# A single-core hybrid HGRN2 / Conformer layer: measured durations in the planner's estimate, side taps held back while a root is pending, statistics delayed, final_g loaded with the last split of weights

## The chip, the cores and the metric

One core of one Trainium2 chip. The metric is the device time of one execution in microseconds, as the median of several runs. A profiled execution gives the rows that are quoted here.

## The reference

One decoder layer and a final norm, in float32, for 2048 new prompt tokens (16 meta tokens go ahead of them; their rows are dropped from the output) and one new token for each of 8 running sequences:

```python
hn = rmsnorm(h, norm1_g)
q_r, f_r, i_r, g_r, a_r, b_r = split(hn @ w_in)            # 1024 -> 4 x 512 and 2 x 512
f = lb + (1 - lb) * sigmoid(f_r)
o = hgrn2(silu(q_r), 1 - f, i_r, log(f))                   # 4 heads of 128 x 128 state, gated recurrence
y_hg = rmsnorm(o, hg_onorm_g) * silu(g_r)
glu = a_r * sigmoid(b_r)
y_cv = silu(layernorm(depthwise_conv31(glu) + conv_b))     # 512 channels
h = h + concat(y_hg, y_cv) @ w_out
h = h + square(relu(rmsnorm(h, norm2_g) @ w_up)) @ w_down  # 1024 -> 4096 -> 1024
y = rmsnorm(h, final_g)
```

The outputs are y for the prompt and for the samples, and the new recurrent and convolution states of both.

## The kernel before

Tokens lie along the free dimension of the matmuls, and channels on the partitions. The float32 products of the projections are formed from three products of parts: each factor is split into a high and a low part (hi and lo), and hi x hi, hi x lo and lo x hi are added in PSUM.

The prompt is cut into four quarters of 512 tokens. The first 950 us or so are a list of units on TensorE: the input projection of a quarter (24 units of 24 matmuls: q, f, v, g for each of four heads, a and b for each of four groups of conv channels) and the output projection of a quarter (8 units of 24 matmuls, one for each 128 of the 1024 columns), in the order in 0, in 1, out 0, in 2, out 1, in 3, out 2, out 3. The epilogue of a unit reads PSUM on ScalarE and VectorE. Then the MLP goes over the tokens in three passes of 680, 688 and 680, each with 16 groups of 256 hidden columns; the up projection of a group is formed from seven products of sums of blocks, and the pieces of the down projection lie between them.

All other work is done by *background generators*, which put their instructions between those of the units:

- `x_pair` and `x_work` (lines 417 and 435) load and transpose the tokens of a half quarter; x_pair finds the row norms (ScalarE squares, a root) and broadcasts them with a matmul of a diagonal tile (`dg`) against ones.
- `hgrn` (line 1002) is the chunked recurrence of one head in one quarter: a scan and a reciprocal on VectorE, transposes, score and state matmuls on PE, a root for the head's norm, a scaling on ScalarE (tile KPn), its transposes, and the split of the result into hi and lo. `hgrn_sample` does the samples.
- `conv` and `conv_part` (lines 1194 and 1206) add 31 taps for each channel group. VectorE takes taps from the front of the list into PSUM (`ps<-glu,cw,ps`), and the *side* takes them from the back: ScalarE multiplies (`acc<-glu,cw`) and POOL adds (`acc<-acc`). `ln_tiles` (line 1285) is the LayerNorm behind it.
- `out_store` (line 1438) stores a finished column block of h and adds up its squares (tile fg: ScalarE squares, POOL adds); behind the last block a matmul of ones with the sum (`fg,ones` on PE) gives the statistics of the MLP's norm. `h_first` and `h_rest` prepare the MLP's input.
- `finish` and `finish_last` (lines 1719 and 1750) end the MLP for up to 128 tokens: PE transposes the sum (`ident,acc`) into two PSUM banks, ScalarE adds up the squares (tile junk), POOL forms the root, VectorE scales with `final_g` (`xn<-ps,kept,fg`), which frees the banks.

A *root* is `rsqrt` (line 333): one VectorE operation, then a power on POOL (`kept<-stat,mhalf`), then back to the users.

Where a generator's steps come between the units is fixed when the program is built, by a planner. Every instruction goes through `Proxy.call` (lines 106 to 149; all show as line 147 in the profile), which adds an estimated cost to the clock of its engine in `Model`. A generator yields the name of the engine that its next step needs, and `Background.ready` (line 184) lets it go on when the estimate says so: a PE step when its inputs will be ready 60 ns before PE comes to it, a step of another engine when that isn't planned over 600 ns ahead, and a side tap when ScalarE and POOL aren't planned over 1500 ns ahead. Where a unit can't go on without a result, `Background.until` forces the steps that are left. The estimate sets the order only; on the chip the engines wait for each other by semaphores.

In the MLP, `d_load` and `d_split` (lines 1884 and 1900) load the down weights and split them in the first pass; the splits are kept in HBM (down_w) for the other passes. `to_store` holds DMA issues on SP back to a later unit. The tile `fg` takes a part of these weights while they are split, so final_g can be loaded into it only behind that.

## Time and profile before

| | before |
|---|---|
| median of 3 runs | 2393.43 us (2393.3 to 2396.77) |
| profiled execution, its own time | 2392.3 us |
| its span, first to last instruction | 2390.6 us (1.7 us lie around it) |
| mean granted clock of TensorE | 0.984 |
| busy: PE / DVE / ACT / POOL | 2280.4 / 1631.1 / 1047.1 / 693.4 us |

In the profile, PE is TensorE, DVE VectorE, ACT ScalarE, POOL GpSimd and SP SyncE. A row of the timeline says when an operation starts, how long it and those of its kind right behind it take, what it writes and reads (out<-in, the program's names without buffer numbers), its shape, and in brackets how long the engine idled before it, and on whom. A view of waits adds up such idle time by what ended it. The granted clock is the share of full speed at which TensorE may run.

### The profile page before, as it was taken

The numbers are of one execution on the slowest core, as the hardware profiler recorded it, in microseconds if no ns is written. First come the engines' busy times: TensorE is split into PE (matmuls) and PEld (weight loads), VectorE is DVE, ScalarE is ACT, GpSimd is POOL, SyncE is SP. The second block draws the span as 40 slices with busy tenths as digits, with TensorE's granted clock in tenths as the row PEclk, the third lists the DMA queues.
The fourth block names the chain that finished last, engine by engine and source line by source line (L and its number), as shares of the span: only waits on it lengthen the run. The fifth ranks groups of instructions, "written<-read, shape, count | busy, mean of one in ns | idle before, by whom it ended". The sixth has DMA issues, their size and how long they took to land.

```text
span 2390.6 us, 36863 instructions
## 1 busy us (share of the span) xinstructions
PE 2280.4 (95%) x13790; PEld 2141.5 (90%) x13790; DVE 1631.1 (68%) x2550; ACT 1047.1 (44%) x2195; POOL 693.4 (29%) x555
## 2 busy tenths in 40 slices
PE   8988989999998998999999998999999989999998
PEld 7987778878877886899999997999999989999998
DVE  5896977387559445577777765787776558666665
ACT  6543744454246242644554444344443353333332
POOL 4652543444147022253333331211111013100000
PEclk9998999999999999999999999999999999999999
DMA  8765445944664457456666575455554755333332
GB/s 298 243 209 168 171 182 176 329 161 158 208 216 163 143 212 261 136 182 185 200 201 195 166 241 183 156 166 173 169 164 122 235 177 162 111 110 111 111 110 108
DMA packets 309466, 428.68 MB, mean 179 GB/s; under 512 B 21506, under 2 KB 216391, under 8 KB 292896
## 3 DMA queue, kind: packets, MB, share of 16 engines
q1 hardware_dynamic: 309144, 426.06, 55.2%
q8 instruction: 109, 1.79, 0.3%
q14 instruction: 69, 0.57, 0.1%
q10 hardware_dynamic: 144, 0.26, 0.0%
HBM read 311.75 MB, written 114.97 MB: 179 GB/s over the span
## 4 chain that ended last, share of the span: by engine, by line
PE 61%; DVE 12%; DMA 5%; issue 4%; ACT 4%; POOL 1%; SPq 1%; POOLq 0%; ACTq 0%; DVEq 0%
PE ps L147 61%; DVE ps L147 4%; ACT cst L147 1%; DVE raw L147 1%; DVE cst L147 1%; SPq L147 1%; ACT wsp L147 1%; DMA xscr<-acc 1%; DVE acc L147 1%; DMA bst<-in_w_up_dram 1%; DMA junk<-in_w_down_dram 1%; DMA fg<-in_w_down_dram 1%; POOL wsp L147 1%; DMA bop_d<-stg 1%; DMA down_w<-wsp 1%
## 5 line engine op out<-in xcount | busy, mean ns | idle before, releaser
L147 PE MATMUL ps<-op,wsp 128*128 128x512 f32 (+6 forms) x5427 | 1051.3, 348 | 13.9 <-DVE glu L147 6.3
L147 PEld LDWEIGHTS ps<-op,wsp 128*128 128x128 f32 x5427 | 884.6, 192 | 116.0 <-issue 11.1
L147 PE MATMUL ps<-hid,wsp 128*128 128x344 f32 (+2 forms) x4512 | 762.7, 320 | 13.3 <-ACT wsp L147 4.7
L147 PEld LDWEIGHTS ps<-hid,wsp 128*128 128x128 f32 x4512 | 716.1, 188 | 20.9 <-ACT wsp L147 10.6
L147 DVE TENSOR_TENSOR acc<-ps,acc 128x688 f32<-128x688 f32 (+4 forms) x416 | 341.7, 823 | 315.9 <-PE ps L147 264.7
L147 ACT ACTIVATE cst<-cst 128x344 f32<-128x344 f32 (+1 forms) x384 | 188.9, 492 | 504.7 <-DVE cst L147 498.2
L147 PE MATMUL ps<-op,ups 128*128 128x344 f32 (+1 forms) x2013 | 351.0, 323 | 4.3 <-DVE ups L147 1.7
L147 PEld LDWEIGHTS ps<-op,ups 128*128 128x128 f32 x2013 | 325.3, 190 | 6.6 <-DVE ups L147 3.1
L147 POOL TENSOR_TENSOR acc<-acc 128x512 f32<-128x512 f32 x165 | 218.1, 1322 | 154.9 <-ACT acc L147 146.8
L147 DVE SCALAR_TENSOR_TENSOR ps<-glu,cw,ps 128x512 f32<-128x512 f32 x299 | 225.3, 753 | 8.7
L147 DVE TENSOR_TENSOR cst<-ps,cst 128x344 f32<-128x344 f32 (+1 forms) x336 | 171.2, 509 | 16.1 <-PE ps L147 12.5
L147 POOL TENSOR_TENSOR ups<-bst,ups 128x512 fp32r<-128x512 f32 x50 | 77.5, 1559 | 335.8 <-ACT ups L147 234.8
L147 DVE TENSOR_TENSOR hid<-cst,hid 128x344 fp32r<-128x344 f32 (+1 forms) x192 | 105.1, 547 | 72.5 <-ACT hid L147 71.7
L147 POOL TENSOR_TENSOR wsp<-bst,wsp 128x512 fp32r<-128x512 f32 x42 | 63.7, 1524 | 255.0 <-ACT wsp L147 229.1
L147 POOL TENSOR_TENSOR kept<-stat,mhalf 128x4 f32<-128x4 f32 (+6 forms) x48 | 38.6, 804 | 331.3 <-DVE stat L147 331.0
L147 POOL TENSOR_TENSOR wsp<-fg,wsp 128x256 fp32r<-128x256 f32 x84 | 68.5, 820 | 195.3 <-ACT wsp L147 177.2
L147 ACT ACTIVATE acc<-glu,cw 128x512 f32<-128x512 f32 x181 | 120.5, 715 | 5.3 <-DVE glu L147 5.3
L147 DVE TENSOR_TENSOR ups<-raw,ups 128x512 fp32r<-128x512 f32 x108 | 81.8, 758 | 31.4 <-ACT ups L147 31.0
L147 POOL TENSOR_TENSOR wsp<-raw,wsp 128x1024 fp32r<-128x1024 f32 (+1 forms) x34 | 79.0, 2323 | 79.8 <-ACT wsp L147 75.0
L147 ACT ACTIVATE hid<-cst 128x344 fp32r<-128x344 f32 (+1 forms) x192 | 94.5, 492 | 6.1
L147 ACT ACTIVATE wsp<-raw 128x512 fp32r<-128x512 f32 (+1 forms) x118 | 86.0, 729 | 14.1 <-DMA raw<-in_w_in_dram 4.6
L147 DVE TENSOR_TENSOR raw<-raw,bst 128x512 f32<-128x512 f32 x92 | 79.2, 861 | 3.2 <-DMA bst<-in_w_up_dram 1.6
(246 smaller groups left out, 2080.9 us busy)
## 6 DMA issues: line engine op xcount, KB each, us to landing
wsp<-kw SPq DMA_DIRECT2D x96, 1024.0 KB
wsp<-down_w SPq DMA_DIRECT2D x248, 256.0 KB
bst<-in_w_up_dram SPq DMA_DIRECT2D x138, 256.0 KB
kw<-wsp SPq DMA_DIRECT2D x32, 1024.0 KB
down_w<-wsp SPq DMA_DIRECT2D x128, 256.0 KB
bop_d<-stg SPq DMA_DIRECT2D x56, 344.0 KB
raw<-in_w_in_dram SPq DMA_DIRECT2D x24, 512.0 KB
raw<-in_w_up_dram SPq DMA_DIRECT2D x48, 256.0 KB
```

The lines of the kernel that those rows point to most:

```text
L147: return fn(*args, **kw)
```

## The change

It has six parts.

1. The costs in `Proxy.call` become other numbers (n is the number of columns): an operation of VectorE goes from 68 + 1.1 n to 155 + 1.045 n ns, a tap to 205 + 1.05 n, a scan to 60 + 3.0 n, a copy from 65 + 0.53 n to 150 + 0.55 n, an activation from 130 + 0.8 n (and 100 for a scale from a tile) to 175 + 0.8333 n (and 93 for each scale or bias from a tile, 194 for a sum beside it), a POOL operation from 60 + 2.2 n to 190 + 2.17 n.
2. A counter `bg.roots` is raised while `x_pair`, `hgrn` or `ln_tiles` has a root pending; side taps aren't issued as long as it isn't zero.
3. In `out_store`, the matmul of the statistics of the first three quarters is planned 5 us later.
4. In `d_split`, the DMA of `final_g` is issued on SP with the last split, not by way of `to_store`.
5. `conv_sample` gets a lower priority and adds its bias with one operation instead of four.
6. `hgrn_sample` and `conv_sample` yield more often; of this and of a counter in `run_unit` that nothing reads, the diff shows nothing here.

```diff
@@ line 128 @@
                     else:
                         cost = 2.6 + 0.4167 * n
                 elif name == "act":
-                    cost = 130 + 0.8 * n
-                    if not isinstance(kw.get("scale", 1.0), float):
-                        cost += 100
+                    cost = 175 + 0.8333 * n
+                    for x in ("scale", "bias"):
+                        if not isinstance(kw.get(x, 1.0), (float, int)):
+                            cost += 93
+                    if "accum_out" in kw:
+                        cost += 194
                 elif name == "pool" and ALU.pow in args:
                     cost = 400 + 155 * n
                 elif name == "pool":
-                    cost = 60 + 2.2 * n
+                    cost = 190 + 2.17 * n
                 elif f == "reciprocal":
-                    cost = 60 + 6.3 * n
+                    cost = 75 + 6.4 * n
+                elif f == "tensor_tensor_scan":
+                    cost = 60 + 3.0 * n
                 elif f in ("bn_stats", "tensor_reduce"):
-                    cost = 65 + 1.05 * _size(args[1])
+                    cost = 150 + 1.05 * _size(args[1])
                 elif f in ("tensor_copy", "memset"):
-                    cost = 65 + 0.53 * n
+                    cost = 150 + 0.55 * n
+                elif f == "scalar_tensor_tensor" and not isinstance(kw["scalar"], float):
+                    cost = 205 + 1.05 * n
                 else:
-                    cost = 68 + 1.1 * n
+                    cost = 155 + 1.045 * n
                 model.op(name, cost)
             return fn(*args, **kw)
 
@@ line 176 @@
         self.m = model
         self.tasks = []
         self.now = 0.0
+        self.roots = 0
 
     def add(self, gen, prio=5):
         self.tasks.append([gen, Ctx(self.m.cur.t), "poll", prio])
@@ line 191 @@
         if e in ("pe", "sp"):
             return r + self.MARGIN <= now
         if e == "side":
-            return r <= now and max(t["act"], t["pool"]) < now + self.SPARE
+            return not self.roots and r <= now and max(t["act"], t["pool"]) < now + self.SPARE
         return r <= max(t[e], now) and t[e] < now + self.HORIZON
 
     def resume(self, entry):
@@ line 425 @@
         for i, t in enumerate(tiles):
             S.activation(junk16, t[:, 0:D], AF.Square, accum_out=ss[:, i:i + 1])
         yield "dve"
+        bg.roots += 1
         r = yield from rsqrt(ss, 2, 1.0 / D)
+        bg.roots -= 1
         yield from row_bc([r[:, i:i + 1] for i in range(2)], bc_t[:, pr])
         yield from region(1, q - 1)
         left = [2]
@@ line 1097 @@
                     o = ps[:, bo, j * P:(j + 1) * P]
                     T.matmul(o, lhsT=scT[:, j], rhs=vn[:, j], start=True, stop=False)
                     T.matmul(o, lhsT=Qp[:, j * P:(j + 1) * P], rhs=Sch[:, j], start=False, stop=True)
+                bg.roots += 1
                 yield "act"
                 ss = sc(4)
                 for j in range(4):
@@ line 1105 @@
                 rr = yield from rsqrt(ss, 4, 1.0 / P)
                 for j in range(4):
                     S.activation(on[:, j], ps[:, bo, j * P:(j + 1) * P], AF.Copy, scale=rr[:, j:j + 1])
+                bg.roots -= 1
                 banks.give(bo)
                 yield "pe"
                 bt = yield from bank1()
@@ line 1266 @@
                 for c in range(NC4):
                     yield "dve"
                     V.tensor_copy(scv[:, c, :, HALO], gs[:, c])
+                    yield "dve"
                     V.tensor_tensor(scv[:, c], scv[:, c], cw[:, c].unsqueeze(1).to_broadcast([P, NS, TAPS]), ALU.mult)
+                    yield "dve"
                     V.tensor_reduce(dws[:, c], scv[:, c], AX.X, ALU.add)
-                    V.tensor_scalar(dws[:, c], dws[:, c], cb[:, c:c + 1], None, ALU.add)
+                yield "dve"
+                V.tensor_tensor(dws, dws, cb.unsqueeze(2).to_broadcast([P, NC4, NS]), ALU.add)
                 xns.give(sct)
                 yield "pe"
                 b = yield from bank1()
@@ line 1303 @@
                 for i in range(m):
                     V.bn_aggr(mv[:, i], bst[:, i])
                 yield from gap()
+                bg.roots += 1
                 r_ = yield from rsqrt(mv[:, :, 1], m, 1.0, parts=n)
+                bg.roots -= 1
                 nm = keep(m)[:n]
                 V.scalar_tensor_tensor(out=nm, in0=mv[:, :, 0], scalar=-1.0, in1=r_, op0=ALU.mult, op1=ALU.mult)
                 for i, (b, (sl, c0_)) in enumerate(zip(bs, dsts)):
@@ line 1406 @@
                     bg.add(conv(q, c), 4 + q)
                     if c == NC4 - 1:
                         if q == 0:
-                            bg.add(conv_sample(), 1.7)
+                            bg.add(conv_sample(), 2.2)
                         bg.add(ln(q), 1.5)
                         if q == NQ - 1:
                             bg.add(conv_state_out())
@@ line 1456 @@
                         S.activation(sq[:, 0:K8 * NS], hsT.rearrange("p k t -> p (k t)"), AF.Square)
                     if q == NQ - 1:
                         yield from until(("second",))
+                    else:
+                        model.cur.t += 5000.0
                     yield "pe"
                     b = yield from bank1()
                     T.matmul(ps[0:2, b, :], lhsT=ones[:, 0:2], rhs=hsq, start=True, stop=True)
@@ line 1910 @@
                     model.cur = was
                 dn[1] += 1
                 if j == NG * 8 - 1:
-                    to_store[1].append(lambda: SP.dma_start(
-                        fg, final_g.rearrange("(o d) -> o d", o=1).to_broadcast([P, D])))
+                    SP.dma_start(fg, final_g.rearrange("(o d) -> o d", o=1).to_broadcast([P, D]))
 
         to_store = [[], []]
```

Since all costs change, most background steps take other places. Three of these follow, each before and then with the change.

ScalarE, from the end of output quarter 2 to the first preparation of the MLP's input (op, xn and bst belong to that input, hsT to the samples; the last fg<-acc here is the square of the last block of h, on which the statistics matmul rests):

```order
L147 ACTIVATE fg<-acc 128x512 x3
L147 ACTIVATE xn_116<-hsT 128x8
L147 ACTIVATE xn_117<-hsT 128x8
L147 ACTIVATE bst_7051<-xn_116,vec 128x344
L147 ACTIVATE op_83<-xn_116,vec 128x344
L147 ACTIVATE op_83<-bst_7051 128x344
L147 ACTIVATE xn_90<-hsT 128x8
L147 ACTIVATE xn_91<-hsT 128x8
L147 ACTIVATE bst_7052<-xn_90,vec 128x344
L147 ACTIVATE fg<-acc 128x512
L147 ACTIVATE op_83<-bst_7051 128x344
```

```order
L154 ACTIVATE fg<-acc 128x512
L154 ACTIVATE xn_116<-hsT 128x8
L154 ACTIVATE xn_90<-hsT 128x8
L154 ACTIVATE bst_7061<-xn_116,vec 128x344
L154 ACTIVATE op_83<-xn_116,vec 128x344
L154 ACTIVATE xn_91<-hsT 128x8
L154 ACTIVATE xn_117<-hsT 128x8
L154 ACTIVATE bst_7062<-xn_91,vec 128x344
L154 ACTIVATE fg<-acc 128x512
L154 ACTIVATE op_83<-bst_7061 128x344 x2
```

The last square stood behind op<-bst; now it stands ahead of it, behind bst<-xn alone.

PE, from the last head of the last quarter (ident,KPn) through the end of output quarter 2 (op_83) into output quarter 3 (op_84):

```order
L147 MATMUL ps<-ident,KPn 128x128 x4
L147 MATMUL ps<-ident,acc 128x128 x4
L147 MATMUL ps<-op_83,wsp_89 128x512 x3
L147 MATMUL ps<-op_83,wsp_87 128x512 x24
L147 MATMUL ps<-op_83,wsp_88 128x512 x24
L147 MATMUL ps<-op_83,wsp_89 128x512 x24
L147 MATMUL ps<-op_84,wsp_87 128x512 x24
L147 MATMUL ps<-op_84,wsp_88 128x512 x24
L147 MATMUL ps<-op_84,wsp_89 128x512 x24
L147 MATMUL ps<-op_84,wsp_87 128x512 x3
L147 MATMUL ps<-fg,ones 2x512
```

```order
L154 MATMUL ps<-op_83,wsp_89 128x512 x3
L154 MATMUL ps<-ident,KPn 128x128 x4
L154 MATMUL ps<-op_83,wsp_89 128x512 x21
L154 MATMUL ps<-op_84,wsp_87 128x512 x24
L154 MATMUL ps<-op_84,wsp_88 128x512 x24
L154 MATMUL ps<-op_84,wsp_89 128x512 x24
L154 MATMUL ps<-op_84,wsp_87 128x512 x21
L154 MATMUL ps<-fg,ones 2x512
L154 MATMUL ps<-op_84,wsp_87 128x512 x3
```

Between the transposes of the last head and the first matmul of output quarter 3 there were 3 + 24 + 24 + 24 = 75 projection matmuls, and there are 21; the statistics matmul (fg,ones) comes behind 93 instead of 75 matmuls of that quarter.

SP, around the load of final_g (wsp<-down_w loads a split of down weights, down_w<-wsp stores one, op<-bop_d loads input of the MLP, raw and bst take up weights):

```order
L147 DMA down_w<-wsp_87 128x512
L147 DMA wsp_87<-down_w 128x512
L147 DMA op_83<-bop_d 128x2x344
L147 DMA raw_85<-in_w_up_dram 128x4x128
L147 DMA bst_7051<-in_w_up_dram 128x4x128 x2
L147 DMA bst_7052<-in_w_up_dram 128x4x128
L147 DMA down_w<-wsp_87 128x512
L147 DMA fg<-in_final_g_dram 128x1024
```

```order
L154 DMA down_w<-wsp_87 128x512
L154 DMA wsp_87<-down_w 128x512
L154 DMA fg<-in_final_g_dram 128x1024
L154 DMA op_84<-bop_d 128x2x344
L154 DMA down_w<-wsp_87 128x512
L154 DMA wsp_87<-down_w 128x512
L154 DMA op_83<-bop_d 128x2x344
L154 DMA raw_85<-in_w_up_dram 128x4x128
L154 DMA bst_7061<-in_w_up_dram 128x4x128 x2
L154 DMA bst_7062<-in_w_up_dram 128x4x128
L154 DMA down_w<-wsp_87 128x512
L154 DMA wsp_87<-down_w 128x512
```

The load of final_g stood behind four loads of up weights and a store; now it stands ahead of them, right behind a wsp<-down_w.

## Rows read from the trace of the kernel before

**Rows 1.** The page: busy time by engine, share of the span, instructions.

```profile
PE 2280.4 (95%) x13790; PEld 2141.5 (90%) x13790; DVE 1631.1 (68%) x2550; ACT 1047.1 (44%) x2195; POOL 693.4 (29%) x555
```

**Rows 2.** Waits on PE, 0 to 777 us: releaser: us in total, times, longest.

```profile
PE ps L147 <- DVE dg L147: 13.6, 5, 3.2
PE ps L147 <- ACT acc L147: 10.1, 6, 2.5
PE ps L147 <- DVE glu L147: 8.3, 3, 3.9
PE ps L147 <- ACT KPn L147: 7.5, 3, 4.2
PE ps L147 <- DVE xn L147: 4.6, 4, 2.0
```

**Rows 3.** Windows: length, busy of PE, PEld, DVE, ACT, POOL, granted clock, DMA share, GB/s.

```profile
0.00:240.00 240.00, 205.79 (x1514) 197.95 (x1515) 179.52 (x295) 123.07 (x248) 118.96 (x86) 0.93 0.71 229
240.00:780.00 540.00, 510.79 (x2688) 426.41 (x2687) 380.86 (x614) 262.77 (x555) 244.28 (x182) 0.99 0.56 195
...
1440.00:1468.00 28.00, 19.18 (x105) 18.20 (x105) 15.23 (x24) 11.42 (x22) 5.85 (x6) 0.83 0.62 212
```

**Rows 4.** Groups by form, 0 to 960 us: busy us, mean ns | idle before.

```profile
L147 PE MATMUL ps<-op,wsp 128*128 128x512 f32 x2304 | 566.0, 401 | 0.0
L147 DVE SCALAR_TENSOR_TENSOR ps<-glu,cw,ps 128x512 f32<-128x512 f32 x299 | 225.3, 753 | 8.7
...
L147 DVE COPY kept<-I 128x4 f32<-128x4 f32 x16 | 8.1, 504 | 0.0
```

**Rows 5.** Timeline near 55 us: start us, us, operation, count [idle before <-releaser].

```profile
52.37 2.33 DVE L147 SCALAR_TENSOR_TENSOR ps<-glu,cw,ps 128x512 f32<-128x512 f32 x3
...
55.88 1.22 DVE L147 TENSOR_SCALAR dg<-ident,kept 128x128 f32<-128x128 f32 x2
...
56.96 0.71 PE L147 MATMUL ps<-dg,ones 128*128 128x128 f32 x4 [2.32 <-DVE dg L147]
```

**Rows 6.** Timeline near 195 us.

```profile
192.78 2.66 POOL L147 TENSOR_TENSOR acc<-acc 128x512 f32<-128x512 f32 x2 [3.89 <-ACT acc L147]
...
196.88 1.25 PE L147 MATMUL ps<-ident,KPn 128*128 128x128 f32 x4 [4.19 <-ACT KPn L147]
...
209.67 0.17 DVE L147 COPY kept<-I 128x4 f32<-128x4 f32 x1
```

**Rows 7.** Timeline near 147 us.

```profile
147.44 2.63 POOL L147 TENSOR_TENSOR wsp<-raw,wsp 128x1024 fp32r<-128x1024 f32 x1 [0.23 <-ACT wsp L147]
147.72 2.38 DVE L147 COPY kept<-I 128x4 f32<-128x4 f32 x1
```

**Rows 8.** Timeline, statistics of the third quarter.

```profile
908.31 0.59 ACT L147 ACTIVATE bst<-xn,vec 128x344 f32<-128x344 f32 x1 [12.33 <-DMA xn<-hscr]
...
916.95 0.49 ACT L147 ACTIVATE op<-bst 128x344 fp32r<-128x344 f32 x1 [7.58 <-DVE bst L147]
...
920.23 1.87 PE L147 MATMUL ps<-fg,ones 128*2 128x512 f32 x2 [4.22 <-POOL fg L147]
```

**Rows 9.** Timeline, SP, ahead of the transfer of final_g.

```profile
1430.99 0.32 SPq L147 DMA_DIRECT2D wsp<-down_w  x1
```

**Rows 10.** Timeline, final_g and the first bank of finish.

```profile
1437.92 0.56 POOL L147 TENSOR_TENSOR kept<-stat,mhalf 128x1 f32<-128x1 f32 x1 [7.10 <-DVE stat L147]
...
1439.45 0.43 SPq L147 DMA_DIRECT2D fg<-in_final_g_dram  x1
...
1444.93 1.28 DVE L147 SCALAR_TENSOR_TENSOR xn<-ps,kept,fg 128x1024 f32<-128x1024 f32 x1 [7.09 <-DMA fg<-in_final_g_dram]
...
1446.27 1.97 PE L147 MATMUL ps<-ident,acc 128*128 128x128 f32 x8 [5.65 <-DVE xn L147]
```

**Rows 11.** Timeline of the tail.

```profile
2373.95 1.02 ACT L147 ACTIVATE junk<-ps 40x1024 bf16<-40x1024 f32 x1 [0.83 <-ACT junk L147]
...
2378.87 1.27 DVE L147 SCALAR_TENSOR_TENSOR xn<-ps,kept,fg 40x1024 f32<-40x1024 f32 x1
```

More of the change, by code (lines that the diff above doesn't have):

```diff
@@ L682, in tile_hybrid_step @@
     pend = [None, None]
+    unit = [0]
     def run_unit(gen, epilogue):
         first = True
+        unit[0] += 1
+        done.add(("unit", unit[0]))
         for _ in gen:
@@ L1268, in conv_sample @@
                     V.tensor_copy(scv[:, c, :, HALO], gs[:, c])
+                    yield "dve"
                     V.tensor_tensor(scv[:, c], scv[:, c], cw[:, c].unsqueeze(1).to_broadcast([P, NS, TAPS]), ALU.mult)
+                    yield "dve"
                     V.tensor_reduce(dws[:, c], scv[:, c], AX.X, ALU.add)
-                    V.tensor_scalar(dws[:, c], dws[:, c], cb[:, c:c + 1], None, ALU.add)
+                yield "dve"
+                V.tensor_tensor(dws, dws, cb.unsqueeze(2).to_broadcast([P, NC4, NS]), ALU.add)
                 xns.give(sct)
```

## The prediction

> **What bounds the kernel now.** I read the engine totals first: PE is busy 95% of the run and no other engine over 68% [rows 1], so the time is PE's work plus the stretches in which it waits or runs at the lower clock. The list of waits on PE comes next, for the time up to 777 us. The costliest five kinds all end on an operation of VectorE or ScalarE, at most 4.2 us at a time [rows 2]: these engines deliver late, and no transfer does. The windows say where they lie [rows 3]. In the first 240 us PE is busy 205.8, so it idles 34.2; from 240 to 780 us it idles 540 - 510.8 = 29.2. That is 63.4 us of idle time in the input and output projections. The granted clock there is 0.93 and 0.99 of full speed, which is about 0.07 x 240 + 0.01 x 540 = 22 us of full-speed time, a part of it while PE was idle. In the 28 us in which the first pass of the MLP ends, PE is busy 19.2 and the clock is 0.83: 8.8 us idle and 4.8 us of clock. The rest of the MLP has little to give, and the change does nothing for it.
>
> Last, I read single stalls in the timeline, to see why the late engine was late.
> - Near 55 us PE waits 2.32 us for the diagonal tile that broadcasts the row norms of x_pair [rows 5]. Its two VectorE operations stand behind three taps of 2.33 us together and more of the same. The planner counted a tap at 68 + 1.1 x 512 = 631 ns, and it takes 753 [rows 4], so six taps in a row put VectorE 0.7 us behind the plan, and nothing in the plan gives that back.
> - Near 195 us the power that ends the rsqrt of an HGRN head waits on POOL behind two side-tap adds of 2.66 us, and PE waits 4.19 us for KPn [rows 6].
> - The statistics of the third quarter wait 4.22 us [rows 8]: the last square on ScalarE stood behind an operation that waited 7.58 us for VectorE, which for its part waited for a DMA. The square itself needed none of that.
> - At the end of the first MLP pass, VectorE waits 7.09 us for final_g and PE 5.65 us for the bank that it empties [rows 10].
>
> **The change, part by part**, against the profiled execution of 2392.3 us; the median of the runs is 1.1 us above it.
>
> *Measured costs.* No operation is removed; the planner now places each PE step of the background later, where the measured times let it be ready, and fills the time until then with projection matmuls. (1) Waits on dg: 13.6 us in five [rows 2]. A tap now counts 743 ns against 753, so the lag of rows 5 is gone; I take 11 off and leave one. (2) Waits on acc from ScalarE, 10.1 us, and on xn, 4.6 us, are steps of x_work, of the heads and of hgrn_sample that came later than planned. They are of the same kind, but their VectorE operations contend with POOL (below), so I take 9 of these 14.7, between 0 and all. (3) Waits on glu, 8.3 us, lie in epilogues of the main stream that the program doesn't let wait: kept, 1 us off.
>
> *Root gate.* It forbids side taps while a power is pending. Its clean case is rows 6, 4.19 us. The stalls on KPn are 7.5 us in three. At the first head of the first quarter the planner is still forced to wait for a root, so I take 3 off. The cost is held-back taps: ScalarE and POOL must do them later. Both idle much more than half of the run, and there the cost is nothing; if that cover goes, a conv channel ends late and its LayerNorm with it.
>
> *New places, new stalls.* All these steps come 2 to 20 us later in the stream, nearer to what needs them. At the start of the last output quarter (the PE rows of the change above) the transposes of the last head had 75 projection matmuls of cover, and have 21 now. At 566.0 us / 2304 = 0.246 us each [rows 4] that is 18.4 us before and 5.2 after. I charge 3 us for stalls of this kind; the bounds are 0, if the plan is right, and one stall of the longest kind seen, 4.2, in each of four quarters, 17.
>
> *Clock.* The clock falls to its lower level (1.2 GHz instead of 2.4) behind stalls, so fewer stalls give some back: I take 7 of the 22 us [rows 3], since 21 of the 63 us idle go.
>
> Sum to 780 us: -11 - 9 - 1 - 3 + 3 - 7 = -28.
>
> *Statistics delayed.* The matmul comes 18 projection matmuls later, 18 x 0.246 = 4.4 us, just over the 4.22 us stall. The last square now stands on ScalarE ahead of the operation that waited 7.58 us, and can run behind the one at 908.31 [rows 8]. Two reasons, each enough: -4.2, and with the clock, which was at its lower level behind this stall, -6.
>
> *final_g.* Its transfer took from 1439.45 to 1444.93, that is 5.48 us [rows 10]. Now it stands on SP right behind a load that was issued at 1430.99 [rows 9] instead of behind four loads of MLP weights and a store. From 1431.4 it lands by about 1436.9, before the power ends at 1438.5 (1437.92 + 0.56). VectorE's 1.28 us then end near 1439.8, and PE's stall had begun at 1446.27 - 5.65 = 1440.6: all of the 5.65 goes, and about 2 of 4.8 us of clock. What is queued behind on SP starts 0.43 us later each; VectorE is idle 7 us there, so this costs nothing. In sum -7.5. Late next is the second bank, as before.
>
> *Tail.* The finish of the last 40 rows moves late: its square, 1.02 us [rows 11], now stands between the squares of the last columns on ScalarE, and its scaling, 1.27 us, ahead of two of VectorE's last products. Nothing covers this, since in the last microseconds PE has no more work: 1.02 + 1.27 = +2.3 us at most, taken whole.
>
> *The rest*: a conv_sample that adds its bias once instead of four times, and more places at which the generators yield: zero, within 1 us either way, hidden by PE's matmuls.
>
> Sum: 2392.3 - 28 - 6 - 7.5 + 2.3 = 2353.1; with the 1.1 us to the median about **2354**.
>
> **Port contention, the rule that speaks against the new costs.** Near 147 us a copy of 128x4 on VectorE takes 2.38 us while POOL runs a subtraction of 2.63 [rows 7]; alone it takes 0.17 [rows 6], and its mean is 504 ns [rows 4]. The new formula counts 150 + 0.55 x 4 = 152 ns. So a number from measured means, and even more one from quiet operations, misses a meeting of the two engines, which costs 2.38 - 0.17 = 2.2 us. The Trainium skill (SBUF — State Buffer, section on who interferes with whom) says why: VectorE and GpSimd share a pair of ports, and one blocks the other for a whole instruction. By that rule the taps, with one operand in SBUF, aren't held up, but the chain of a head is, and better constants can't mend it; rows 7 agree.
>
> **Rivals.**
> 1. *The stalls move* (by contention). Sixteen heads each run a chain of some ten VectorE operations beside POOL. If nine of them meet a POOL operation on the path at 2.2 us, 20 of the 28 us up to 780 us are back. For it: rows 7; against it: rows 4, where the mean of that copy is only 0.33 us above its quiet time. Time: 2354 + 20 = 2374.
> 2. *Nearly all goes*: the whole 63.4 us but the forced waits (glu and the start, some 14), and 15 of the 22 of clock. That is 49 + 15 = 64 where the forecast has 28: 2354 - 36 = 2318. Against it: xn and acc stalls that were there through contention.
> 3. *It doesn't do what it says*: the order moves, but every stall comes back elsewhere, since forced waits set them, and the tail and new waits eat the 13.5 of statistics and final_g as well: 2390 to 2396.
> 4. *Slower: the end of each quarter comes late.* The place is the first unit of an output quarter, which needs the last head's result in its second half. Its price is all by which that chain overruns the 5.2 us of matmuls now before it, on PE with nothing to fill it. To undo 39 us and end over 2398, the four quarters have to overrun by 44, 11 us each. For it: cover shrank from 75 matmuls to 21. Against it: the longest stall of this kind was 4.2 us [rows 6], and four of those make 17. Its time, with 12 us each: 2354 + 48 = 2402.
>
> **How the numbers follow.** A measurement of this kernel can tell about 0.2%, 4.8 us, from no change. The forecast has 0.56, rival 1 0.20, rival 2 0.06, rival 3 0.09, rival 4 0.09. Faster: 0.56 + 0.20 + 0.06 = 0.82; same 0.09; slower 0.09. The forecast's own range is 2338 to 2366: down by half of what is left of the waits on acc, xn, KPn and of the clock, some 16, up by most of the 14 by which new stalls may reach their bound of 17. The whole range leaves out rivals 3 and 4 and the most of rival 2, 2 in 10 in all. It reaches down to 2328, half-way and more to rival 2, and up to 2386, rival 1 with 12 of those 14 us.
>
> **What would show it.** In the profile of the changed kernel: no wait on dg over 2 us; KPn once or twice; the matmul of the third quarter's statistics without a gap and the clock at 1.0 around it; no wait of VectorE on final_g, and no gap near 1440; the last microseconds behind PE's final matmul 2 us longer than before. PE idle to 780 us near 42 us instead of 63, and its clock in the first 240 us about 0.95. The forecast is wrong if PE idles 55 us or more there, or if waits appear at the start of the output quarters.

## The result and the profile after

The changed kernel takes 2357.33 us (median of 4 runs, 2356.18 to 2359.21), against 2393.36 us for the kernel before in the same comparison: a ratio of 0.985, with a 95% interval of 0.9833 to 0.9867. The forecast was 2354, with a range of 2328 to 2386. Its profiled execution took 2359.21 us, with a span of 2357.5, which is 33.1 us less than before.

The page of the changed kernel, engine totals, which answer to [rows 1]:

```profile
span 2357.5 us, 36896 instructions
...
PE 2272.0 (96%) x13790; PEld 2136.6 (91%) x13790; DVE 1642.6 (70%) x2531; ACT 1052.1 (45%) x2208; POOL 719.5 (31%) x571
```

The windows of the changed kernel, which answer to the first two of [rows 3] (length, busy PE, PEld, DVE, ACT, POOL, granted clock):

```profile
0.00:240.00 240.00, 214.27 (x1570) 205.02 (x1571) 192.21 (x297) 127.61 (x261) 131.29 (x94) 0.95 0.73 240
240.00:780.00 540.00, 528.86 (x2784) 442.34 (x2782) 396.56 (x618) 272.13 (x575) 257.69 (x189) 0.99 0.57 199
```

Up to 780 us PE idles 25.7 + 11.1 = 36.9 us instead of 63.4; I had said near 42. The waits on PE in that time, which answer to [rows 2]:

```profile
PE ps L154 <- ACT KPn L154: 7.2, 2, 5.4
PE ps L154 <- DVE F L154: 4.6, 1, 4.6
PE ps L154 <- DVE dg L154: 4.1, 2, 2.7
PE ps L154 <- ACT acc L154: 3.4, 2, 2.8
PE ps L154 <- DVE QS L154: 3.4, 1, 3.4
PE ps L154 <- DVE glu L154: 3.1, 2, 2.0
PE ps L154 <- ACT xn L154: 2.7, 1, 2.7
```

Two kinds that [rows 2] leave out stood in the kernel before with these totals (F and QS are tiles of the heads):

```profile
PE ps L147 <- DVE F L147: 3.3, 1, 3.3
PE ps L147 <- DVE QS L147: 1.0, 1, 1.0
```

The waits on dg fell from 13.6 to 4.1 us, those on acc from 10.1 to 3.4 and those on glu from 8.3 to 3.1; those on KPn stayed, and those on F and QS grew by 3.7. Both kernels issue the same 12480 matmuls of the projections and the MLP, so the start of the same matmul in both traces shows where the time was won (in us, counted from 0, worked out from the start times in the traces):

```
matmul   before    after     difference
   960    177.16   165.60    -11.55
  1440    320.88   296.51    -24.36
  2400    549.82   525.24    -24.58
  3360    818.24   785.14    -33.10
  3840    951.37   914.96    -36.41   end of output quarter 3
  4320   1044.42  1018.11    -26.31   start of the MLP is over
  6720   1434.22  1406.81    -27.42
  6960   1494.41  1458.86    -35.55   first pass is over
 12479   2381.21  2346.59    -34.62   last matmul
```

Small steps of such a table say little: in the run with final_g alone, below, PE, VectorE, ScalarE and POOL do the same in the same order as in the kernel before, and yet its matmul 4320 starts 4.2 us later. So three things happened: 36 us were won up to the end of the output projections, 10 of them were given back at the start of the MLP, and 8 were won at the end of the first pass. What the prediction has no term for is the second. The timeline of the changed kernel there:

```profile
913.80 0.32 SPq L154 DMA_DIRECT2D hscr<-vn  x1
...
914.40 0.38 SPq L154 DMA_DIRECT2D raw<-in_w_up_dram  x1
914.84 1.66 SPq L154 DMA_DIRECT2D acc<-in_w_up_dram  x3
916.54 0.50 SPq L1515 DMA_DIRECT2D scT<-xscr  x1
...
921.09 0.69 DVE L154 TENSOR_TENSOR scT<-ps,scT 128x512 f32<-128x512 f32 x1 [6.12 <-DMA scT<-xscr]
...
921.70 0.57 DVE L154 SCALAR_TENSOR_TENSOR op<-xn,vec,op 128x344 fp32r<-128x344 f32 x1
...
922.32 4.09 PE L154 MATMUL ps<-op,ups 128*128 128x344 f32 x13 [6.09 <-DVE op L154]
```

In the kernel before nothing waits for scT:

```profile
944.92 0.37 SPq L1492 DMA_DIRECT2D scT<-xscr  x1
...
953.47 0.68 DVE L147 TENSOR_TENSOR scT<-ps,scT 128x512 f32<-128x512 f32 x1
```

scT is the residual of the last column block. Its load now stands on SP behind a store and four loads of up weights, VectorE waits 6.12 us for it, and the inputs of the first MLP products (op) stand behind it on VectorE, in program order.

The end of the first pass went as forecast. It answers to [rows 10]:

```profile
1403.92 1.10 SPq L154 DMA_DIRECT2D fg<-in_final_g_dram  x1
...
1411.09 1.28 DVE L154 SCALAR_TENSOR_TENSOR xn<-ps,kept,fg 128x1024 f32<-128x1024 f32 x1 [0.67 <-POOL kept L154]
...
1413.53 1.04 PE L154 MATMUL ps<-ident,acc 128*128 128x128 f32 x8
```

VectorE now waits for the root, 0.67 us, and not for final_g, and PE finds the bank free without a gap. Its next wait for a bank of finish is 1.82 us, at 1418.7 us.

### The profile page after: what moved, and what is told of

It reads as the page before. It is cut to its first block, busy times and chain, and to the rows that moved or that the text cites. A ratio compares the mean times of both kernels' runs of the same rounds, so it can differ in the third digit from the quotient of the medians.

```text
span 2357.5 us, 36896 instructions
## 1 busy us (share of the span) xinstructions
PE 2272.0 (96%) x13790; PEld 2136.6 (91%) x13790; DVE 1642.6 (70%) x2531; ACT 1052.1 (45%) x2208; POOL 719.5 (31%) x571
## 4 chain that ended last, share of the span: by engine, by line
PE 70%; DVE 12%; DMA 6%; issue 5%; ACT 3%; POOL 2%; SPq 1%; POOLq 0%; ACTq 0%; DVEq 0%
PE ps L154 70%; DVE ps L154 2%; DMA down_w<-wsp 1%; ACT cst L154 1%; DVE raw L154 1%; SPq L154 1%; DVE cst L154 1%; DVE I L154 1%; POOL wsp L154 1%; DVE acc L154 1%; DVE xn L154 1%; DMA bst<-in_w_up_dram 1%; DMA fg<-in_w_down_dram 1%; DVE B L154 1%; DMA xscr<-acc 1%
## 5 line engine op out<-in xcount | busy, mean ns | idle before, releaser
L154 POOL TENSOR_TENSOR acc<-acc 128x512 f32<-128x512 f32 x178 | 241.5, 1357 | 157.5 <-ACT acc L154 148.6
L154 DVE SCALAR_TENSOR_TENSOR ps<-glu,cw,ps 128x512 f32<-128x512 f32 x286 | 215.1, 752 | 7.7
L154 POOL TENSOR_TENSOR wsp<-bst,wsp 128x512 fp32r<-128x512 f32 x42 | 63.4, 1518 | 257.7 <-ACT wsp L154 211.2
L154 ACT ACTIVATE acc<-glu,cw 128x512 f32<-128x512 f32 x194 | 130.5, 716 | 1.0 <-DVE glu L154 1.0
L154 ACT ACTIVATE junk<-ps 128x128 bf16<-128x128 f32 (+3 forms) x86 | 36.7, 427 | 111.1 <-PE ps L154 108.6
```

The costliest lines, as they stand in the source:

```text
L154: return fn(*args, **kw)
```

## The experiments

**Four of the six parts alone.** Each run is the kernel before with one part of the change. Parts 5 and 6 (conv_sample and the places to yield) weren't run alone. First the costs (the whole table of `Proxy.call`):

```diff
-                    cost = 130 + 0.8 * n
+                    cost = 175 + 0.8333 * n
...
-                    cost = 68 + 1.1 * n
+                    cost = 155 + 1.045 * n
```

> The kernel before with the new costs alone. Forecast: the measured costs carry the projections: main matmuls at the end of output quarter 3 some 20 to 28 us earlier than before, whole time 2365 to 2373 us; waits of PE on dg gone or once. The wait for final_g (5.6 us) stays. If the gate and the delayed statistics do the work instead: within 5 us of before (2388 or more).

Measured: 2391.9 us against 2392.84, ratio 0.999 (0.998 to 1.0). So the costs, which carried half of my forecast (21 of 39 us), give nothing alone. The timeline shows what eats them (POOL, then PE):

```profile
283.44 13.71 POOL L154 TENSOR_TENSOR acc<-acc 128x512 f32<-128x512 f32 x10 [1.81 <-ACT acc L154]
...
297.11 1.53 POOL L154 TENSOR_TENSOR kept<-stat,mhalf 8x1 f32<-8x1 f32 x2
...
299.79 0.59 PE L154 MATMUL ps<-ident,acc 8*128 8x8 f32 x4 [11.71 <-ACT acc L154]
```

Ten side adds, 13.71 us, stand on POOL ahead of two roots, and PE waits 11.71 us for what hangs on them. By the starts of the matmuls this run is 17.2 us ahead of the kernel before at matmul 960 and 1.2 behind at 1440, so what was won goes in the stretch with this wait. Waits on dg did shrink, as expected, to 4.6 us. PE has no gap at the third quarter's statistics (915.1 us): the costs alone remove that stall.

The gate alone:

```diff
-            return r <= now and max(t["act"], t["pool"]) < now + self.SPARE
+            return not self.roots and r <= now and max(t["act"], t["pool"]) < now + self.SPARE
```

> The kernel before with side taps held back while a root is pending, alone, at the old costs. Forecast: the waits on KPn shrink from 7.5 us to about 4, 2388 to 2392 us. Rival, held-back taps make conv channels late: 2394 to 2400 us, with waits on acc or at the start of output quarters.

Measured: 2390.69 us, ratio 0.9987 (0.9977 to 0.9997): a small gain, as expected. Up to 777 us the waits on KPn are 2.5 us instead of 7.5, but PE now waits 4.6 us for a_t, which it didn't before.

The delay of the statistics alone:

```diff
+                    else:
+                        model.cur.t += 5000.0
```

> The kernel before with the statistics of the first three quarters planned 5 us later, alone. Forecast: PE's 4.2 us wait at the third quarter's statistics goes, and with it a stretch at the lower clock: 5 to 6 us earlier at the end of output quarter 3. What is left of it at the end of the run tells whether the start of the MLP gives it back: 2387 to 2389 us if nothing is given back, 2392 to 2394 if all is.

Measured: 2395.7 us, ratio 1.0009 (1.0 to 1.0019). All is given back, and perhaps a little more. The windows show both, first of the kernel before, then of this run:

```profile
918.00:928.00 10.00, 7.77 (x20) 4.83 (x21) 8.70 (x19) 6.43 (x14) 1.44 (x2) 0.66 0.73 230
928.00:1000.00 72.00, 64.18 (x309) 54.60 (x308) 50.74 (x79) 37.50 (x81) 21.86 (x18) 0.93 0.47 140
```

```profile
918.00:928.00 10.00, 9.94 (x40) 6.90 (x40) 7.72 (x15) 5.59 (x14) 1.46 (x1) 1.00 0.95 322
928.00:1000.00 72.00, 56.72 (x262) 49.80 (x261) 52.10 (x82) 34.07 (x73) 18.26 (x14) 0.88 0.45 138
```

At 918 us the stall and the lower clock are gone (PE busy 9.94 of 10 us, clock 1.00). Then PE waits in the 72 us behind: busy 56.72 instead of 64.18.

The early load of final_g alone:

```diff
-                    to_store[1].append(lambda: SP.dma_start(
-                        fg, final_g.rearrange("(o d) -> o d", o=1).to_broadcast([P, D])))
+                    SP.dma_start(fg, final_g.rearrange("(o d) -> o d", o=1).to_broadcast([P, D]))
```

> The kernel before with the early load of final_g alone. Forecast: 7 to 8 us faster (2385 to 2387 us), the wait of 5.65 us at the end of the first pass gone. Rival, the second bank of finish takes the place of the first: a gain under 3 us (2390 or more). The order up to 1000 us is the same, so the projections show no difference.

Measured: 2386.36 us, 6.5 less than before, ratio 0.997 (0.9959 to 0.9981): the forecast, within its interval. The four parts alone add up to 0.9 + 2.2 - 2.9 + 6.5 = 6.7 us, of the 36 that the whole change gives.

**Costs and gate together**, on the kernel before:

> The kernel before with the new costs and the gate together, no other part. Alone, the costs gave 0.9 us and the gate 2.2. Theory 1: the two work only together, since the new costs let the planner queue ten side adds on POOL ahead of a root (one wait of 11.7 us in the run with the costs alone) and the gate forbids that: 2362 to 2370 us, no wait over 6 us up to 780 us. Theory 2: parts add up: 2387 to 2391 us, and the rest of the gain needs the delayed statistics.

Measured: 2368.11 us against 2394.2, ratio 0.9888 (0.9872 to 0.9905). Theory 1 holds: 0.9 and 2.2 us apart, 26.1 together, and no wait over 5.2 us up to 780 us. With the 6.5 us of final_g that makes 32.6 of the 36.0 us; the 3.4 that are left for the delay and for parts 5 and 6 are no more than the intervals leave open.

**The changed kernel without the gate**, its counter left out of the condition:

```diff
-            return not self.roots and r <= now and max(t["act"], t["pool"]) < now + self.SPARE
+            return r <= now and max(t["act"], t["pool"]) < now + self.SPARE
```

> The changed kernel without the gate: side taps are issued while a root is pending. Theory 1: it loses 20 to 30 us against the changed kernel (2377 to 2388 us), with waits on KPn, acc or dg behind a run of adds on POOL. Theory 2: it loses 2 to 4 us (2359 to 2362), what the gate gave alone.

Measured: 2366.7 us, ratio 0.9887 (0.9873 to 0.9902), so about 9 us slower than the changed kernel (8.5 by the gains over the kernel before, each in its own comparison). This lies between the two theories. The mechanism is there (timeline; POOL, then PE):

```profile
291.74 3.95 POOL L154 TENSOR_TENSOR acc<-acc 128x512 f32<-128x512 f32 x3 [0.51 <-ACT op L154]
295.65 1.02 POOL L154 TENSOR_TENSOR kept<-stat,mhalf 128x4 f32<-128x4 f32 x1
...
297.12 1.25 PE L154 MATMUL ps<-ident,KPn 128*128 128x128 f32 x4 [7.34 <-ACT KPn L154]
```

but with three adds ahead of the root, not ten. How many pile up depends on the rest of the order. By the starts of the matmuls this run is 4.6 us ahead of the changed kernel at matmul 960 and 22.5 behind at 1440, a stretch with this wait and others in it; by 1920 it is 9.6 behind, at the last matmul 6.9, and what gives the 13 us back isn't shown. So the gate is what makes the costs pay on the kernel before. That the whole change needs it isn't so: without the gate the rest still gives 27.5 us.

**The changed kernel without the delay of the statistics:**

> The changed kernel with the statistics of the first three quarters at their old time. Theory: what the delay saves at the third quarter's statistics is given back at the start of the MLP, where VectorE and the transfers ahead of it set the time: within 3 us of the changed kernel either way (2354 to 2361 us), later before 920 us and less waiting from 920 to 950. Rival, the delay is a gain of its own as forecast: 2362 to 2364 us.

Measured: 2363.54 us, ratio 0.987 (0.9855 to 0.9884), 6 us slower than the changed kernel by the medians and 5 by the gains; the two intervals overlap. The rival's time, but not at the rival's place: PE has no gap at the third quarter's statistics here either (890.1 us). At the end of output quarter 3 this run has lost only 4.5 us against the changed kernel, and it lost 7.1 of its own between the matmuls 1920 and 2400, near 477 us:

```profile
474.18 2.60 POOL L154 TENSOR_TENSOR acc<-acc 128x512 f32<-128x512 f32 x2
474.25 1.21 DVE L154 SCALAR_TENSOR_TENSOR kept<-stat,kept 128x2 f32<-128x2 f32 x1 [2.71 <-POOL kept L154]
475.39 1.48 DVE L154 TENSOR_SCALAR dg<-ident,kept 128x128 f32<-128x128 f32 x2
...
476.79 0.15 DVE L154 TENSOR_SCALAR fg<-ps 1x8 f32<-1x8 f32 x1
...
476.99 1.22 PE L154 MATMUL ps<-dg,ones 128*128 128x128 f32 x4 [3.82 <-DVE fg L154]
```

The row names fg<-ps, VectorE's reading of the samples' statistics, as the end of PE's wait. But dg, which PE's product takes in, ended at 476.87 us, not 0.1 us before fg<-ps did, so without fg<-ps PE would have waited nearly as long. It waits for VectorE, which waited for a root and then took 1.21 and 1.48 us for two steps beside side adds on POOL; in the changed kernel these take 0.15 and 0.47. With the delay this crowd has another order and PE doesn't wait here; that the delay itself brings this about, and not the new order as such, isn't shown.

**The last residual loaded first**, on the changed kernel; only one row of SP moves:

```diff
-                    out_load(q, t)
+                    if (q, t) not in res_of:
+                        out_load(q, t)
+                    if q == NQ - 1 and t == 6:
+                        out_load(q, 7)
```

> The changed kernel with one transfer moved on SP: the last block's residual (scT) is loaded right behind the one ahead of it, not behind a store and four loads of up weights. Theory: VectorE waits 6.1 us for it in program order with the MLP's inputs behind it, so PE's wait of 6.1 us at 922 us falls to 2 us or less: 2351 to 2354 us. Rival, the MLP's inputs are late for other reasons too (ScalarE, the up weights): the wait moves on to the next products, within 2 us of the changed kernel.

Measured: 2353.92 us, ratio 0.983 (0.9815 to 0.9844), 3.4 us less than the changed kernel, with intervals that overlap. The order on PE, VectorE, ScalarE and POOL is the same in both. From matmul 3840 to 4320 this run gives back 6.2 us where the changed kernel gives back 10.1, so the gain lies where it should. The timeline:

```profile
903.83 0.40 SPq L1515 DMA_DIRECT2D scT<-xscr  x1
...
910.59 0.69 DVE L154 TENSOR_TENSOR scT<-ps,scT 128x512 f32<-128x512 f32 x1
```

VectorE doesn't wait for scT any more, and PE's longest wait at the first products is 1.36 us instead of 6.09. It is a part of the 10 us that are given back; of the next waits on op behind it, one grew (from 3.62 to 4.70 us) and one stayed (1.37).

**POOL's long subtractions in four pieces**, on the changed kernel. These form the low parts of the in and out weights:

```diff
-            G.tensor_tensor(w[:, 1], r, w[:, 0].bitcast(F32), ALU.subtract)
+            for k in range(0, w.shape[-1], 256):
+                G.tensor_tensor(w[:, 1, k:k + 256], r[:, k:k + 256], w[:, 0, k:k + 256].bitcast(F32), ALU.subtract)
```

It tests rival 1. In the changed kernel, the longest wait on KPn, 5.42 us, comes with this row beside it:

```profile
177.16 2.34 POOL L154 TENSOR_TENSOR wsp<-raw,wsp 128x1024 fp32r<-128x1024 f32 x1 [6.83 <-ACT wsp L154]
177.22 2.32 DVE L154 TENSOR_TENSOR aux<-aux,vec 128x32 f32<-128x32 f32 x1
...
181.83 1.25 PE L154 MATMUL ps<-ident,KPn 128*128 128x128 f32 x4 [5.42 <-ACT KPn L154]
```

> The changed kernel with each POOL subtraction that forms the low part of in and out weights (128x1024, 2.3 to 2.9 us) cut into four of 256 columns. If VectorE is held up until POOL's operation ends, a meeting now costs some 0.6 us instead of up to 2.6: the VectorE operations of 2.3 to 2.6 us (copies, 128x4 and 128x32 sums) go, and PE's waits on acc, xn, KPn and QS up to 780 us (16.7 us in the changed kernel) lose 6 to 10 us: 2346 to 2352 us. Rival, the waits are the planner's and not the port's: the same waits, and 17 us more work on POOL (four starts in place of one, some 0.19 us each, 90 times) makes it 2357 to 2363 us.

Measured: 2338.37 us, ratio 0.9757 (0.9732 to 0.9781), 19 us less than the changed kernel (22 by the gains) and more than I had expected. Since the planner counts four POOL operations, the order of everything else moves too. The next run settles which of the two it is.

**The same order with whole subtractions.** The planner counts four, and one is issued. The sequence of instructions on PE, VectorE, ScalarE and SP is the same in both, and that on POOL too but for the pieces:

```diff
-                G.tensor_tensor(w[:, 1, k:k + 256], r[:, k:k + 256], w[:, 0, k:k + 256].bitcast(F32), ALU.subtract)
+                model.op("pool", 190 + 2.17 * 256)
+            nc.gpsimd.tensor_tensor(w[:, 1], r, w[:, 0].bitcast(F32), ALU.subtract)
```

> The order of instructions of the run with POOL's subtractions in four pieces (the planner counts four), but each subtraction issued as one instruction of 1024 columns. If long POOL operations hold VectorE up, the waits come back: 2350 to 2358 us, and the quiet-and-blocked operations of VectorE are as long as in the changed kernel. Rival, the four counts gave a better order and nothing else: 2335 to 2341 us.

Measured: 2356.07 us, ratio to the kernel before 0.9842 (0.9824 to 0.9861), where the pieces had 0.9757 (0.9732 to 0.9781). The gain over the changed kernel is gone but for 3 us, which the intervals don't tell from nothing, so it came from the pieces and not from the order. The timelines show the same two VectorE operations, first with whole subtractions, then in pieces:

```profile
98.50 2.84 POOL L675 TENSOR_TENSOR wsp<-raw,wsp 128x1024 fp32r<-128x1024 f32 x1
99.01 2.36 DVE L154 COPY kept<-I 128x4 f32<-128x4 f32 x1
...
133.78 3.33 POOL L675 TENSOR_TENSOR wsp<-raw,wsp 128x1024 fp32r<-128x1024 f32 x1
134.83 2.32 DVE L154 TENSOR_TENSOR_SCAN B<-F,ones 128x16 f32<-128x16 f32 x1
```

```profile
89.10 2.32 POOL L154 TENSOR_TENSOR wsp<-raw,wsp 128x256 fp32r<-128x256 f32 x2
90.75 0.70 DVE L154 COPY kept<-I 128x4 f32<-128x4 f32 x1
...
126.98 2.20 POOL L154 TENSOR_TENSOR acc<-acc 128x512 f32<-128x512 f32 x1
128.02 1.21 DVE L154 TENSOR_TENSOR_SCAN B<-F,ones 128x16 f32<-128x16 f32 x1
```

The copy is held up to 2.36 us by a whole subtraction and 0.70 us by a piece; alone it takes 0.17 [rows 6]. The scan meets a whole subtraction in the one run and a side add in the other. Up to 960 us VectorE's operations, the same ones in the same order, take 739.0 us with whole subtractions and 722.6 with pieces (added up from the traces), and the 301 taps of 512 columns among them 226.6 and 226.5. Yet the pieces are more work for POOL. Their groups by form in the two runs (busy us, mean ns):

```profile
L675 POOL TENSOR_TENSOR wsp<-raw,wsp 128x1024 fp32r<-128x1024 f32 x30 | 73.9, 2463 | 53.6 <-ACT wsp L154 50.1 <-DMA kw<-wsp 1.8 <-PE ps L154 1.5
```

```profile
L154 POOL TENSOR_TENSOR wsp<-raw,wsp 128x256 fp32r<-128x256 f32 x120 | 94.0, 814 | 43.4 <-ACT wsp L154 41.1 <-PE ps L154 2.3
```

**The bias of conv_sample as before**, four operations with one tensor operand in place of the one of 2.32 us above:

```diff
+                    V.tensor_scalar(dws[:, c], dws[:, c], cb[:, c:c + 1], None, ALU.add)
...
-                V.tensor_tensor(dws, dws, cb.unsqueeze(2).to_broadcast([P, NC4, NS]), ALU.add)
```

> The changed kernel with the bias of conv_sample added by four operations with one tensor operand, as before, instead of one with two. In the changed kernel that one took 2.32 us beside a POOL subtraction (0.2 us of work) ahead of a head's root, and PE then waited 5.42 us for KPn. Theory of the ports: that wait falls by 1.5 to 2.2 us, 2353 to 2356 us. Rival, the plan's order around it decides: the wait stays within 0.7 us, 2356 to 2359 us.

Measured: 2364.29 us, ratio 0.9861 (0.9834 to 0.9889), 7 us slower than the changed kernel by the medians and 4 by the gains, with intervals that overlap. Neither theory said slower. The wait on KPn is 6.67 us now, and new waits of 1.7 to 4 us stand at 300, 390 and 439 us, far from the edit. The subtraction meets another operation of VectorE there, a copy that takes 0.17 us when nothing holds it up (at 173.11 us in the changed kernel):

```profile
176.54 2.38 POOL L154 TENSOR_TENSOR wsp<-raw,wsp 128x1024 fp32r<-128x1024 f32 x1 [6.42 <-ACT wsp L154]
176.63 2.32 DVE L154 COPY xn<-glu 128x8 f32<-128x8 f32 x1
```

So the edit didn't take the meeting away, and the run doesn't test what it was meant to test. What it does show is that one small edit can bring new waits far from its place through the planner. The 9 and 5 to 6 us of the runs without the gate and without the delay have to be read with that in mind.

**Pieces and residual together**, on the changed kernel:

> POOL's subtractions in four pieces and the last residual loaded first, both on top of the changed kernel: the two gains, 18 to 19 and 3 to 4 us, lie at different places and add up: 2333 to 2337 us, with no wait over 2 us between 890 and 910. Rival, the start of the MLP gives the second back: 2337 to 2340 us.

Measured: 2332.42 us (2331.16 to 2335.53), ratio to the kernel before 0.9742 (0.9728 to 0.9757). That is 62.9 us less than the kernel before, where the pieces alone gave 57.7: the two gains add up as far as the intervals can tell, and this version beats both kernels. One expectation failed: waits on op at the start of the MLP are still 8.9 us, up to 4.0.

```profile
0.00:240.00 240.00, 231.74 (x1688) 219.85 (x1689) 197.60 (x331) 136.03 (x282) 144.51 (x160) 0.98 0.79 261
240.00:780.00 540.00, 527.84 (x2791) 441.10 (x2790) 390.51 (x616) 261.46 (x558) 248.26 (x202) 1.00 0.57 197
```

PE idles 8.3 + 12.2 = 20.4 us up to 780 us, where the kernel before had 63.4 and the changed one 36.9.

## Why the prediction was right, and where it wasn't

The time was right within 3.3 us, in part by luck. Up to 780 us the forecast was -28. The windows give 26.5 us less idle time and 3.4 us less lost to the clock, and matmul 3360, at 785 us, starts 33.1 us earlier. Behind that the forecast had -6 - 7.5 + 2.3 = -11.2, and the two profiled executions have nothing: the end of the span is 33.1 us earlier, too. A gain that was 5 us larger ahead and a gain of 11 us that is missing behind made a total near the forecast. The steps inside it:

- *Measured costs* (-11, -9 and -1, as a gain of their own) failed. Alone they give 0.9 us. The forecast took the waits that better costs remove, and left out a wait that they make: with the new costs and no gate, ten adds queue up ahead of two roots. In the whole change the kinds of waits moved about as said: dg by -9.5 us, though one of 2.7 is left where none over 2 was to be; acc by -6.7 and xn from VectorE by -4.6, with a new one of 2.7 on xn from ScalarE. Those on glu, which were kept but for 1 us, fell by 5.2.
- *Root gate* (-3) was right in size for the gate alone, 2.2 us, and wrong for the change. On the kernel before it is the part that lets the new costs pay, 26.1 us together instead of 3.1. In the change it is worth 9 us, and not by the waits on KPn, which fell from 7.5 to 7.2. I sized the two parts each against the kernel before, and added; the parts interact, and that was the wrong step. Why the planner lets ten adds through I read only in the code (a forced wait moves its notion of now ahead, which opens the way for side taps); it wasn't tried.
- *New places, new stalls* (+3): the waits on F and QS grew by 3.7 us, and PE waits nowhere at the start of output quarter 3. Rival 4 is out: 21 matmuls of cover were enough.
- *Clock* (-7): half of what was said. Up to 780 us the clock was at its lower level for 34.1 us instead of 41.0, which is 3.4 us of full-speed time; the gain lies in the first 240 us, where the granted clock went from 0.93 to 0.95.
- *Statistics delayed* (-6): the stall at the third quarter went, and its clock, as said, but the new costs remove it without the delay, so it can't be counted twice. The delay alone removes it, too, and the start of the MLP takes that back in full. What the delay is worth in the changed kernel, 5 to 6 us if it is more than a chance of the order, comes for the most part from another place, near 477 us, which the prediction doesn't mention. The size was right by accident.
- *final_g* (-7.5): right for the kernel before, 6.5 alone, and 27.42 to 35.55 in the table, 8.1 us. In the change it is less: the run with costs and gate still has the late load, and gains 4.1 us between the same matmuls 6720 and 6960, so that about 4 of the 8.1 are left for the load.
- *Tail* (+2.3): right. From the start of PE's very last matmul, a transpose, to the end of the span it is 9.93 us instead of 7.96, so +2.0.
- *The rest* (zero, within 1): wrong by 10 us, the step that has no term. At the start of the MLP, 10 us are given back. The load of scT, moved on a queue, has a part in it: the prediction went through what SP carries behind final_g, and not through what it carries here. The run with the residual first gets 3.4 us of it back. But scT isn't the whole cause: without the delay VectorE doesn't wait for scT, and 8.7 us are given back all the same, with waits of 3.73, 4.73 and 4.23 us on VectorE's steps; with the costs alone 9.7. Why these are late is open.
- *The range*: "some 16" for half of what is left of the waits on acc, xn, KPn and of the clock is 12.6 by its own terms (5.7, 4.5 and 15); the time fell on the other side.

*Rival 1, contention*, had a chance of 0.20 as a rival, and was in truth at work beside the forecast. It didn't take 20 us back from the gain, but it held 18 us that the change left lying. The rule of the Trainium skill (SBUF — State Buffer, section on who interferes with whom) that a GpSimd operation that reads SBUF and a VectorE operation with two inputs in SBUF, or a copy in a mode that takes both ports, block each other for the whole instruction agrees with the runs: in the same order, 2356.07 us with operations of 2.46 us on POOL, and 2338.37 with pieces of 0.81, while the taps, with one input in SBUF, take 753 ns in both. "Better constants can't mend it" was right; that the length of POOL's operations could was not in the prediction.

## What to carry to other kernels

Two parts of a planner can each be worth next to nothing alone and 26 us together: try parts together, and the whole with one left out, and don't add up what each gives alone. A stall that is taken away pays only if the next thing on the way is early too, so look at what the engine meets next, here the first inputs of the MLP. And where GpSimd works beside a VectorE chain that something waits for, cut its long operations into pieces, even at a quarter more work: the chain waits for one piece instead of the whole.

## What was unexpected

- Cutting 30 POOL operations into 120 raised their time from 73.9 to 94.0 us, and took 17.7 us off the kernel with everything else in the same order (2356.07 to 2338.37; as ratios to the kernel before, each in its own comparison, 0.9842 and 0.9757).
- A copy of four columns, 0.17 us alone, took 2.36 us beside a whole subtraction: a mean of a form (504 ns) hides the few long ones, and a long one can stand in a chain that PE waits for.
- Four small operations in place of one in a side branch (the bias of conv_sample) brought new waits of 1.7 to 4 us at three places far away, through the planner, and left the wait that the edit was aimed at in place.
